# Ten modulation units of a two-layer diffusion block: column layout and VectorE sums in place of float32 products

## The chip, the cores and the metric

One Trainium2 chip, one core of it. The metric is the device time of one execution in microseconds; the kernel before takes 1705.74 us, the median of 3 runs (1704.96 to 1706.06). Five engines work side by side, each through its own queue in order: TensorE (matrix products; PE in the profile, its weight loads PEld), VectorE (DVE), ScalarE (ACT), GpSimd (POOL) and SyncE (SP), which here issues every load from HBM.

## What is computed

Two layers of a hybrid diffusion block on 256 latent tokens and 256 context tokens of width 1024. In each layer a vector c (and another one, c_ctx, for the context) gives six shift, scale and gate vectors of width 1024:

```python
c_act = jax.nn.silu(c)
cc_act = jax.nn.silu(c_ctx)
sh1, sc1, g1, sh2, sc2, g2 = jnp.split((c_act @ ada_w[i] + ada_b[i])[:, None, :], N_ADA, axis=-1)
csh1, csc1, cg1, csh2, csc2, cg2 = jnp.split(cc_act @ ada_w[i] + ada_b[i], N_ADA, axis=-1)
...
x_new = x + g1 * merge_groups(p, attn, *group_w)
x_new = x_new + g2 * ffn(modulate(x_new, norm2_g[i], sh2, sc2))
```

Normalized and modulated tokens pass one input projection, whose columns go to four mixers (a chunked spatial gate, pooling, attention with low-rank queries and keys, a Fourier mixer); their outputs are projected back and added with the gate g1. A second normalization, modulated with sh2 and sc2, feeds a dense SwiGLU in layer 0 and a SwiGLU with the best 2 of 8 experts in layer 1, added with g2. Context is carried through layer 0 only. `ada_w` is 1024x6144 float32 per layer, multiplied by two vectors.

## The kernel before, in words

Everything is float32. Large products are made as three products of float32r halves (`mm3`, lines 245 to 248): a weight tile is split into a high part, copied by ScalarE (line 236), and a low part, subtracted by VectorE (line 238). There are three pairs of split tiles in layer 0, and three raw tiles of 1 MB (`raw_unit`, line 229) into which SyncE loads weights in turn.

**The modulation.** `ada_w` of a layer is cut into 24 units of 256 columns, 1 MB each. Units 0 to 7 are sh1 and sc1, 8 to 11 g1, 12 to 15 sh2, 16 to 19 sc2, 20 to 23 g2. In layer 0 a unit is `ada0_unit` (lines 348 to 360): eight float32 products of 32x256, whose weights are 32 columns with c and c_ctx in the first two (`c32`), in four groups of rows of one PSUM bank (line 353); a copy to SBUF on ScalarE (356); two products with a selecting matrix that add the groups and turn the result to columns (358); a small bias add on VectorE (359). Each float32 product shows as two records in the trace. The tile comes from `ada0_load` (332 to 346): among units 8 to 19 the odd ones take a raw tile, the even ones a tile of their own, `aw` (line 815), loaded at line 345; units 20 to 23 take the one buffer `rx` (`ada_raw`, line 838).

In layer 1 a unit is `ada1_unit` (856 to 866). Its weights are laid out with output columns on partitions. `cast_c` (847 to 854) writes c and c_ctx, repeated on all partitions, into `cb` by 16 transposes of broadcast columns (852) and four copies. One VectorE instruction then multiplies a 128x1024 half of a unit by one of the two vectors and sums along the row into one column of `ada` (863): four for units 0 to 7, two for the others, which need no context. Their products go to a throw-away tile `junk`. A small add of the bias follows (866).

**Order of the work.** The program text gives a list; a planner simulates the engines and sets the order on each of them, by priority, which is by default the place in the text, raised where `high_priority` or `pri` stands. In layer 0 units 0 to 7 belong to the first normalization. Then come key and query preparation, `aw`, and a `merge` (line 818) of the latent attention's steps, at raised priority, with a list of other work: units 8 and 9, the input projections `w0_v` and `w0_u`, units 10 and 11, the gate, `w0_z`, `w0_d`, the Fourier mixer, units 12 and 13, 16 to 19, the context's queries, 14 and 15, pooling. The output projections `wout` follow, for the latents and then for the context beside its attention. The dense feed-forward (`ffn`, 868) runs over 14 chunks of 256 hidden columns, for the latents and then for the context; a chunk has 96 products for gate and up and 48 for the chunk before going down. In the first run `cast_c` is hung on chunk 0, units 20 to 23 on chunks 3 to 6, and layer 1's units 0 to 7 on chunks 3 to 10; layer 1's other units are hung on the second run. Small tiles come from pools with a set number of buffers (`temps`; `sm`), among them `t1` (normalized values, squares, the units' copies), `rs`, `gs` and `mx`.

Layer 1's mixers and its experts follow; the experts' weights, 336 units of 1 MB, make up the last half of the time. Their first loads go to tiles that layer 1 sets free.

Of the kernel before, what the change touches and what calls it, by code (L numbers as in the profile page):

```python
# [10 lines left out]
F32 = mybir.dt.float32  # L11
# [87 lines left out]
def _layout(i):  # L99
# [5 lines left out]
    for l in range(2):  # L105
# [54 lines left out]
        else:  # L160
            w = w.reshape(4, 2, 128, 1024)[[3, 0, 1, 2]].transpose(0, 2, 1, 3)
        a[f"wout{l}"] = w.reshape(4, 128, 2048)
    a["ada0"] = i["ada_w"][0].reshape(8, 128, 24, 256).transpose(2, 1, 0, 3).reshape(24, 128, 2048)
    a["ada1"] = i["ada_w"][1].T.reshape(24, 2, 128, 1024).transpose(0, 2, 1, 3).reshape(24, 128, 2048)

    def units(g, u, d, fm):
# [18 lines left out]
def build(tc, I, out):  # L185
# [125 lines left out]
    def t4(name, shape=(128, 4, 256)):  # L311
        return tt("t4", name, shape)
# [14 lines left out]
        return TB(name, shape)  # L327

    adaw = {}
    aw = None  # L330

    def ada0_load(u, tiles=None):

        if tiles is None:
            if u < 20:
                tiles = [raw_unit(I["ada0"][u])] if u < 8 or u % 2 else [aw]
            else:
                tiles = [ada_raw(I["ada0"][u])]
            load = u > 7 and u < 20 and u % 2 == 0
        else:  # L340
            load = True
        n = 2048 // len(tiles)
        if load:
            for i, t in enumerate(tiles):
                nc.sync.dma_start(t, I["ada0"][u][:, i * n:i * n + n])
        return [t[:, a:a + 256] for t in tiles for a in range(0, n, 256)]

    def ada0_unit(u):
# [8 lines left out]
        for m in range(2):  # L357
            PE.matmul(ps[:, 256 + 2 * m:258 + 2 * m], sb[:, m * 128:m * 128 + 128], C("sel", 0, 2), start=True, stop=True)
        V.tensor_tensor(out=ada[0][:, 2 * u:2 * u + 2, :], in0=ps[:, 256:260].rearrange("p (m i) -> p m i", m=2),
                        in1=ps_(0, "adab", 2 * u, 2)[:, :, None].to_broadcast([128, 2, 2]), op=ALU.add)  # L360

    def rstd(ss, n, dim):
        ms = sm.tile([128, 8], F32, tag="ms", name="ms")
        V.tensor_scalar(ms[:, :n], ss, 1.0 / dim, EPS, op0=ALU.mult, op1=ALU.add)
        r = sm.tile([128, 8], F32, tag="rs", bufs=12, name="rs")
        G.tensor_tensor(out=r[:, :n], in0=ms[:, :n], in1=C("neghalf", 0, n), op=ALU.pow)
        return r

# [26 lines left out]

    def modulate(l, n, jsh, jsc, s, R, kts, hi, lo=None):
        a, w = kts[0], len(kts)
        g = sm.tile([128, 8], F32, tag="gs", bufs=6, name="gs")
        V.scalar_tensor_tensor(g[:, :w], ada[l][:, jsc * 8 + a:jsc * 8 + a + w, s], 1.0, ps_(l, n, a, w), op0=ALU.add,
                               op1=ALU.mult)  # L400
        for i, kt in enumerate(kts):
            t_ = t1("nm")
            V.scalar_tensor_tensor(t_, xs[s][:, kt], g[:, i:i + 1], R, op0=ALU.mult, op1=ALU.mult)
            sh = adav(l, jsh, kt, s)
            S.activation(hi[:, kt], t_, AF.Identity, bias=sh)
            if lo is not None:
                V.scalar_tensor_tensor(lo[:, kt], t_, sh, hi[:, kt].bitcast(F32), op0=ALU.add, op1=ALU.subtract)
# [127 lines left out]
    def attend(st, keys):  # L535

        nk = 2 * len(keys)
        pts = {}

        def soft(h, t):  # L540
            sc = PSC()
            for i, ks in enumerate(keys):
                PE.matmul(sc[:, i * 256:i * 256 + 256], st.qT[:, h, t * 128:t * 128 + 128], ks.kT[:, h, :],
                          start=True, stop=True)
            m = sm.tile([128, 6], F32, tag="mx", bufs=6, name="mx")
            V.tensor_reduce(out=m[:, 0:1], in_=sc[:, :nk * 128], axis=AX.X, op=ALU.max, negate=True)
            p = tb("p")
            S.activation(p[:, :nk * 128], sc[:, :nk * 128], AF.Exp, bias=m[:, 0:1], accum_out=m[:, 1:2])
            V.reciprocal(m[:, 2:3], m[:, 1:2])
            V.tensor_scalar(p[:, :nk * 128], p[:, :nk * 128], m[:, 2:3], None, op0=ALU.mult)  # L550
            tr = PTR()
            for k in range(nk):
                PE.transpose(tr[:, k * 128:k * 128 + 128], p[:, k * 128:k * 128 + 128], ident)
            pts[h] = tb("pt", (128, 4, 128))
            S.activation(pts[h][:, :nk], tr.rearrange("p (k q) -> p k q", k=4)[:, :nk], AF.Copy)

        def soft2(pr, t):

            sc = PSC()
            for j in range(2):  # L560
                PE.matmul(sc[:, j * 256:j * 256 + 256], st.qT[:, 2 * pr + j, t * 128:t * 128 + 128],
                          keys[0].kT[:, 2 * pr + j, :], start=True, stop=True)
            m = sm.tile([128, 6], F32, tag="mx", bufs=6, name="mx")
            V.tensor_reduce(out=m[:, 0:2], in_=sc.rearrange("p (j k) -> p j k", j=2), axis=AX.X, op=ALU.max,
                            negate=True)
            p = tb("p")
            for j in range(2):
                a = slice(j * 256, j * 256 + 256)
                S.activation(p[:, a], sc[:, a], AF.Exp, bias=m[:, j:j + 1], accum_out=m[:, 2 + j:3 + j])
            V.reciprocal(m[:, 4:6], m[:, 2:4])  # L570
            p2 = p.rearrange("p (j k) -> p j k", j=2)
            V.tensor_tensor(out=p2, in0=p2, in1=m[:, 4:6, None].to_broadcast([128, 2, 256]), op=ALU.mult)
            tr = PTR()
            for k in range(4):
                PE.transpose(tr[:, k * 128:k * 128 + 128], p[:, k * 128:k * 128 + 128], ident)
            pt = tb("pt", (128, 4, 128))
            S.activation(pt.rearrange("p k q -> p (k q)"), tr, AF.Copy)
            for j in range(2):
                pts[2 * pr + j] = pt[:, 2 * j:2 * j + 2]

        def mix(pr, t):
            o = PTR()
            for k in range(nk):
                v = keys[k // 2].v
                for j in range(2):
                    h = 2 * pr + j
                    PE.matmul(o[64 * j:64 * j + 64, :128], v[:, k % 2, h * 64:h * 64 + 64], pts[h][:, k, :],
                              start=k == 0, stop=k == nk - 1, tile_position=(0, 64 * j))
# [145 lines left out]
    NPRE = 3  # L734


    temps("tp0", t4=3, t3=3, t2=8, t1=4, ta=6, tb=3, v=2, R=2)
    TB = lambda name, shape: tt("tb", name, shape)
    weights("w0", 3, 3)
    pb, pb_close = pool("pb", bufs=2, space=PSUM)  # L740
# [71 lines left out]
    q_in0(0, x_, pcq, 0)  # L812
    q_in0(0, c_, pcq, 256)
    q_up(0, x_, True)
    aw = t8("aw", F32, (128, 2048))
    new_mix(x_)
    ada0s = lambda *us: lambda: [ada0_unit(u) for u in us]
    merge(pri(1000, attend(x_, [x_, c_])),
          [ada0s(8, 9), w0_v, w0_u, ada0s(10, 11), lambda: gate_mix(0, x_), w0_z, w0_d, lambda: fourier_mix(0, x_),
           ada0s(12, 13), ada0s(16, 17, 18, 19), lambda: q_up(0, c_, False), ada0s(14, 15), lambda: pool_mix(0, x_)])  # L820
# [9 lines left out]
    pq_close()  # L830


    temps("tp1", t4=3, t3=2, t2=6, t1=3, ta=5, v=2, R=1)
    rx, rx_close = pool("rx", bufs=1, side="left")

    def ada_raw(src):
        r = rx.tile([128, 2048], F32, tag="rx", bufs=1, name="rx")
        nc.sync.dma_start(r, src)
        return r
# [2 lines left out]
    pq, pq_close = pool("pq1", bufs=1, space=PSUM)  # L842
    PW = lambda: pq.tile([128, 512], F32, tag="gu", bufs=2, name="gu")
    fp, fp_close = pool("fp", bufs=2, side="right")
    cb = t8("cb", F32, (128, 2, 1024))

    def cast_c():
        for i in range(2):
            for k4 in range(2):
                ps = PS()  # L850
                for k in range(4):
                    PE.transpose(ps[:, k * 128:k * 128 + 128],
                                 c32[:, k4 * 4 + k, i:i + 1].to_broadcast([128, 128]), ident)
                S.activation(cb[:, i, k4 * 512:k4 * 512 + 512], ps, AF.Copy)

    def ada1_unit(u):

        r = (raw_unit if u > 14 else ada_raw)(I["ada1"][u]).rearrange("p (m k) -> p m k", m=2)
        n = 2 if u < 8 else 1
        for m in range(2):  # L860
            for i in range(n):
                j = r[:, m] if n == 1 else t4("junk", (128, 1024))
                V.scalar_tensor_tensor(j, r[:, m], 1.0, cb[:, i], op0=ALU.mult, op1=ALU.mult,
                                       accum_out=ada[1][:, 2 * u + m, i:i + 1])
        a = ada[1][:, 2 * u:2 * u + 2, :n]
        V.tensor_tensor(out=a, in0=a, in1=ps_(1, "adab", 2 * u, 2)[:, :, None].to_broadcast([128, 2, n]), op=ALU.add)

    def ffn(s, fhl, extra):
        fh, fl = fhl
# [48 lines left out]
    ex0[1] += pri(100, [norm2_c])  # L918
    ex0[0].append(cast_c)
    for u in range(4):  # L920
        ex0[3 + u].append(lambda u=u: ada0_unit(20 + u))
    for u in range(8):
        ex0[3 + u].append(lambda u=u: ada1_unit(u))
    ffn(0, fhl, ex0)
# [573 lines left out]
```

## Time and profile before

| | |
|---|---|
| median of 3 runs | 1705.74 us (1704.96 to 1706.06) |
| the profiled execution | 1704.32 us |
| its span in the trace | 1702.5 us |
| mean granted clock of TensorE | 0.991 of full speed |
| busy: TensorE, its weight loads | 1637.2 us (96%), 1248.4 us (73%) |
| busy: VectorE, ScalarE, GpSimd | 854.0 us (50%), 645.2 us (38%), 32.2 us (2%) |
| chain that ended last | TensorE 76%, transfers 19%, VectorE 3%, ScalarE 1% |

The span is what the trace covers; the execution's own time lies 1.8 us above it. Busy shares are of the whole span and mix stages. Matmuls overlap in the engine's pipeline: a product of 256 columns has a duration of 0.28 us and more, but the next one begins 0.12 us after it, so that costs are read from one start to the next, from the chain, or from counts in a stretch. The same holds in a small measure for VectorE.

### The profile page before, as it was taken

Reading aid. Unit: us, or ns where it says so; the run is one execution under the profiler, and the core shown is the slowest. Engines: PE = TensorE matmul, PEld = TensorE weight load, DVE = VectorE, ACT = ScalarE, POOL = GpSimd, SP = SyncE. Lnnn points to the kernel's source line nnn. Section 1 sums busy time; section 2 is a strip of 40 time slices with the busy share of each in tenths; the row PEclk is TensorE's granted clock in tenths of the full one; section 3 lists DMA queues with packets and bytes.
Section 4 is the critical chain, followed back from the end, with each engine's and each line's share of the span. In section 5 each row is a group of like instructions: output and inputs, shape, how many; then the busy total and the mean of one; then the engine's idle time right before and its main releaser. Section 6 shows DMA issues by size and latency. Waiting matters only on the chain.

```text
span 1702.5 us, 28623 instructions
## 1 busy us (share of the span) xinstructions
PE 1637.2 (96%) x11648; PEld 1248.4 (73%) x11648; DVE 854.0 (50%) x1446; ACT 645.2 (38%) x1026; POOL 32.2 (2%) x31
## 2 busy tenths in 40 slices
PE   7999999999999999999899999999999999989996
PEld 4887889999999999999776555555565655545543
DVE  3545666688766666657673334334343424233411
ACT  4434464444454444455472223223232323222200
POOL 0100000000000000000100000000000000000000
PEclk9999999999999999999999999999999999999999
DMA  9425346778744566654479999999999999999996
GB/s 374 171 100 199 136 174 219 276 278 300 268 170 161 198 248 242 246 186 168 173 298 380 420 418 419 419 418 419 416 418 420 418 417 419 419 419 418 419 418 259
DMA packets 77901, 525.26 MB, mean 309 GB/s; under 512 B 9024, under 2 KB 9152, under 8 KB 18240
## 3 DMA queue, kind: packets, MB, share of 16 engines
q1 hardware_dynamic: 77760, 523.33, 77.5%
q8 instruction: 94, 1.54, 0.4%
q14 instruction: 47, 0.39, 0.1%
HBM read 522.25 MB, written 1.05 MB: 307 GB/s over the span
## 4 chain that ended last, share of the span: by engine, by line
PE 76%; DMA 19%; DVE 3%; ACT 1%; issue 1%; SPq 0%; POOL 0%; DVEq 0%; ACTq 0%; POOLq 0%
PE gu L1395 11%; DMA raw<-in_moe 9%; PE gu L247 9%; PE gu L246 9%; PE gu L248 9%; PE ys L1381 5%; DMA prb<-in_moe 5%; PE acc L247 4%; PE acc L246 4%; PE acc L248 4%; DMA x<-in_moe 2%; PE w L246 2%; PE w L248 2%; PE w L247 2%; PE yd L247 1%; DMA spare<-in_moe 1%
## 5 line engine op out<-in xcount | busy, mean ns | idle before, releaser
L238 DVE TENSOR_TENSOR wl<-raw,wh 128x1024 fp32r<-128x1024 f32 x368 | 446.3, 1223 | 221.8 <-ACT wh L236 215.3
L236 ACT ACTIVATE wh<-raw 128x1024 fp32r<-128x1024 f32 x368 | 384.8, 1057 | 330.5 <-PE gu L247 149.8
L246 PE MATMUL gu<-fh,wh 128*128 128x256 f32 x896 | 254.1, 284 | 0.0
L248 PE MATMUL gu<-fh,wl 128*128 128x256 f32 x896 | 251.3, 281 | 0.0
L247 PE MATMUL gu<-fl,wh 128*128 128x256 f32 x896 | 250.9, 280 | 0.0
L1395 PE MATMUL gu<-raw,es 128*64 128x256 f32 x1488 | 181.3, 383 | 5.0 <-DMA raw<-in_moe 4.8
L1398 ACT ACTIVATE sg<-gu 64x256 f32<-64x256 f32 x84 | 31.6, 376 | 394.8 <-PE gu L1395 388.7
L246 PEld LDWEIGHTS gu<-fh,wh 128*128 128x128 f32 x896 | 168.1, 188 | 4.7 <-issue 4.7
L247 PEld LDWEIGHTS gu<-fl,wh 128*128 128x128 f32 x896 | 168.6, 188 | 2.7 <-issue 2.7
L248 PEld LDWEIGHTS gu<-fh,wl 128*128 128x128 f32 x896 | 168.8, 189 | 1.8 <-issue 1.6
L1399 DVE TENSOR_TENSOR sg<-sg,gu 64x256 f32<-64x256 f32 x84 | 35.7, 424 | 254.1 <-ACT sg L1398 253.7
L1395 PEld LDWEIGHTS gu<-raw,es 128*64 128x64 f32 x1488 | 105.5, 137 | 64.5 <-issue 11.2
L247 PE MATMUL acc<-hl,wh 128*128 128x256 f32 x448 | 124.5, 283 | 0.0
L246 PE MATMUL acc<-hh,wh 128*128 128x256 f32 x448 | 123.8, 283 | 0.0
L248 PE MATMUL acc<-hh,wl 128*128 128x256 f32 x448 | 120.3, 283 | 0.0
L1381 PE MATMUL ys<-raw,hs 128*64 128x512 f32 x424 | 103.6, 603 | 7.3 <-DMA raw<-in_moe 6.1
L247 PE MATMUL gu<-wl,ef 128*128 128x512 f32 x224 | 94.9, 424 | 8.2 <-DVE wl L238 8.1
L246 PE MATMUL gu<-wh,ef 128*128 128x512 f32 x224 | 93.4, 418 | 8.2 <-ACT wh L236 8.2
L248 PE MATMUL gu<-wh,ef 128*128 128x512 f32 x224 | 90.3, 403 | 0.0
L247 PEld LDWEIGHTS acc<-hl,wh 128*128 128x128 f32 x448 | 85.7, 191 | 0.0
L246 PEld LDWEIGHTS acc<-hh,wh 128*128 128x128 f32 x448 | 85.6, 191 | 0.0
L248 PEld LDWEIGHTS acc<-hh,wl 128*128 128x128 f32 x448 | 83.3, 191 | 0.0
(448 smaller groups left out, 2521.9 us busy)
## 6 DMA issues: line engine op xcount, KB each, us to landing
raw<-in_moe SPq DMA_DIRECT2D x223, 1024.0 KB, 17.4
raw<-in_ffn SPq DMA_DIRECT2D x84, 1024.0 KB, 4.9
spare<-in_moe SPq DMA_DIRECT2D x31, 1024.0 KB, 18.2
x<-in_moe SPq DMA_DIRECT2D x28, 1024.0 KB, 19.8
prb<-in_moe SPq DMA_DIRECT2D x27, 1024.0 KB, 18.0
rx<-in_ada SPq DMA_DIRECT2D x19, 1024.0 KB, 4.9
raw<-in_ada SPq DMA_DIRECT2D x18, 1024.0 KB, 4.8
cst<-in_moe SPq DMA_DIRECT2D x27, 512.0 KB, 18.0
```

The source lines that it names most:

```text
L236: S.activation(hi, r, AF.Copy)
L238: V.tensor_tensor(out=lo, in0=r, in1=hi.bitcast(F32), op=ALU.subtract)
L246: PE.matmul(o, wh, rh, start=start, stop=False, **kw)
L247: PE.matmul(o, wh, rl, start=False, stop=False, **kw)
L248: PE.matmul(o, wl, rh, start=False, stop=stop, **kw)
L1381: PE.matmul(yd[0][64 * q:64 * q + 64, :], h[:, m * 64:m * 64 + 64], rs[m][:, q * 512:q * 512 + 512], start=c == 0 and m == 0, stop=c == NC ...
L1395: PE.matmul(ps[64 * q:64 * q + 64, :256], st.e[:, kt], rs[k // 2][:, a:a + 256], start=kt == 0, stop=kt == 7, tile_position=(0, 64 * q))
L1398: S.activation(g[64:], ps[:64, :256], AF.Silu)
L1399: V.tensor_tensor(out=g[64:], in0=g[64:], in1=ps[64:, :256], op=ALU.mult)
```

## The change

Units 8 to 13 and 20 to 23 of layer 0 are laid out by column, as layer 1's are, and computed as those are. The function of layer 1 becomes `ada_cols`, for both layers. Units 14 to 19 stay as they were, and so do 0 to 7. `cast_c` moves up to the place where `aw` was taken, and writes a `cb` tile there; it is still hung on chunk 0 of the feed-forward too, where it takes a new `cb` tile and writes it again. `aw` is gone: units 8 to 19 all take raw tiles. In the mixing stage `junk` has one buffer of its own (`jk`), and there are fewer buffers of `t1`, `rs`, `gs` and `mx`.

```diff
-    a["ada0"] = i["ada_w"][0].reshape(8, 128, 24, 256).transpose(2, 1, 0, 3).reshape(24, 128, 2048)
+    a["ada0"] = np.concatenate(
+        [i["ada_w"][0][:, :2048].reshape(8, 128, 8, 256).transpose(2, 1, 0, 3).reshape(8, 128, 2048),
+         i["ada_w"][0][:, 2048:].T.reshape(16, 2, 128, 1024).transpose(0, 2, 1, 3).reshape(16, 128, 2048)])
+    for u in range(14, 20):
+        a["ada0"][u] = i["ada_w"][0][:, 256 * u:256 * u + 256].reshape(8, 128, 256).transpose(1, 0, 2).reshape(128, 2048)
...
         if tiles is None:
-            if u < 20:
-                tiles = [raw_unit(I["ada0"][u])] if u < 8 or u % 2 else [aw]
-            else:
-                tiles = [ada_raw(I["ada0"][u])]
-            load = u > 7 and u < 20 and u % 2 == 0
+            tiles = [raw_unit(I["ada0"][u])]
...
+    def ada_cols(l, u, src, n):
+        r = src.rearrange("p (m k) -> p m k", m=2)
+        e = V if l == 0 else V
+        for m in range(2):
+            for i in range(n):
+                j = r[:, m] if i == n - 1 else tt(JUNK[0], "junk", (128, 1024))
+                e.scalar_tensor_tensor(j, r[:, m], 1.0, cb[0][:, i], op0=ALU.mult, op1=ALU.mult,
+                                       accum_out=ada[l][:, 2 * u + m, i:i + 1])
+        a = ada[l][:, 2 * u:2 * u + 2, :n]
+        e.tensor_tensor(out=a, in0=a, in1=ps_(l, "adab", 2 * u, 2)[:, :, None].to_broadcast([128, 2, n]), op=ALU.add)
...
-        r = sm.tile([128, 8], F32, tag="rs", bufs=12, name="rs")
+        r = sm.tile([128, 8], F32, tag="rs", bufs=8, name="rs")
...
-        g = sm.tile([128, 8], F32, tag="gs", bufs=6, name="gs")
+        g = sm.tile([128, 8], F32, tag="gs", bufs=4, name="gs")
...
-            m = sm.tile([128, 6], F32, tag="mx", bufs=6, name="mx")
+            m = sm.tile([128, 6], F32, tag="mx", bufs=4, name="mx")
...
-    temps("tp0", t4=3, t3=3, t2=8, t1=4, ta=6, tb=3, v=2, R=2)
+    temps("tp0", jk=1, t4=3, t3=3, t2=8, t1=3, ta=6, tb=3, v=2, R=2)
...
-    aw = t8("aw", F32, (128, 2048))
+    cb = []
+    def cast_c():
+        cb[:] = [t8("cb", F32, (128, 2, 1024))]
...
+    cast_c()
     new_mix(x_)
-    ada0s = lambda *us: lambda: [ada0_unit(u) for u in us]
+    ada0s = lambda *us: lambda: [ada_cols(0, u, raw_unit(I["ada0"][u]), 2) if u < 14 else ada0_unit(u) for u in us]
...
+    JUNK[0] = "t4"
...
     for u in range(4):
-        ex0[3 + u].append(lambda u=u: ada0_unit(20 + u))
+        ex0[3 + u].append(lambda u=u: ada_cols(0, 20 + u, ada_raw(I["ada0"][20 + u]), 2))
```

## Rows read from the trace of the kernel before

**Rows 1.** Table by stretches of the span; the first line names the columns.

```profile
core 0: us, PE busy (x) PEld busy (x) DVE busy (x) ACT busy (x) POOL busy (x), PEclk, DMA share, GB/s
0.00:30.00 30.00, 18.07 (x146) 10.02 (x147) 8.83 (x25) 14.40 (x35) 2.21 (x5) 0.96 0.91 359
...
80.00:130.00 50.00, 50.00 (x404) 44.67 (x403) 20.35 (x53) 18.11 (x38) 3.73 (x4) 1.00 0.23 85
130.00:160.00 30.00, 29.71 (x258) 19.75 (x257) 15.78 (x40) 15.10 (x32) 0.59 (x1) 1.00 0.66 244
...
283.00:358.00 75.00, 75.00 (x658) 72.13 (x658) 52.95 (x80) 31.58 (x44) 0.00 (x0) 1.00 0.75 281
358.00:400.00 42.00, 42.00 (x355) 41.85 (x354) 38.54 (x61) 18.61 (x24) 0.00 (x0) 1.00 0.67 248
...
850.00:1702.50 852.50, 806.58 (x4884) 482.64 (x4882) 314.55 (x496) 242.32 (x356) 0.00 (x0) 0.99 0.98 402
```

**Rows 2.** Chain of waits, first 300 us: start, us, engine, tile, line, count.

```profile
44.77 1.64 DVE nm L403 x4
...
95.59 1.86 PE w L353 x32
99.54 0.34 PE w L358 x4
...
146.77 0.42 DVE df L656
...
150.01 0.61 DVE mx L546
...
229.28 0.87 PE b L852 x8
```

**Rows 3.** Waits of TensorE, 50 to 215 us: us in total, times, longest.

```profile
PE w L358 <- ACT adasb L356: 0.8, 2, 0.5
```

**Rows 4.** Instructions in order of time, VectorE, feed-forward of layer 0: start, duration.

```profile
289.60 1.22 DVE L863 SCALAR_TENSOR_TENSOR junk<-rx,cb 128x1024 f32<-128x1024 f32 x1
...
290.74 1.22 DVE L863 SCALAR_TENSOR_TENSOR junk<-rx,cb 128x1024 f32<-128x1024 f32 x1
...
294.18 1.22 DVE L238 TENSOR_TENSOR wl<-raw,wh 128x1024 fp32r<-128x1024 f32 x1
295.32 0.41 DVE L898 TENSOR_TENSOR sg<-sg,gu 128x256 f32<-128x256 f32 x1
295.65 1.22 DVE L238 TENSOR_TENSOR wl<-raw,wh 128x1024 fp32r<-128x1024 f32 x1
...
306.46 0.16 DVE L359 TENSOR_TENSOR ada<-gu,prs 128x4 f32<-128x4 f32 x1 [2.09 <-PE gu L358]
...
325.21 0.16 DVE L359 TENSOR_TENSOR ada<-gu,prs 128x4 f32<-128x4 f32 x1 [2.09 <-PE gu L358]
...
356.85 1.22 DVE L863 SCALAR_TENSOR_TENSOR junk<-rx,cb 128x1024 f32<-128x1024 f32 x1 [1.38 <-DMA rx<-in_ada]
```

**Rows 5.** Instructions in order of time, SyncE's queue of loads.

```profile
34.24 18.68 SPq L229 DMA_DIRECT2D raw<-in_win  x2
...
62.38 13.36 SPq L229 DMA_DIRECT2D raw<-in_win  x2
...
373.97 0.33 SPq L838 DMA_DIRECT2D rx<-in_ada  x1
...
385.29 0.33 SPq L838 DMA_DIRECT2D rx<-in_ada  x1
```

**Rows 6.** Instructions in order of time, VectorE, mixing stage of layer 0.

```profile
69.94 0.48 DVE L520 TENSOR_SCALAR v<-b,rs 128x256 f32<-128x256 f32 x1 [5.23 <-ACT k L518]
...
74.16 1.23 DVE L238 TENSOR_TENSOR wl<-raw,wh 128x1024 fp32r<-128x1024 f32 x1 [1.38 <-ACT wh L236]
...
96.60 1.23 DVE L238 TENSOR_TENSOR wl<-raw,wh 128x1024 fp32r<-128x1024 f32 x1
```

**Rows 7.** Loads by line, first 300 us: count, KB, median us to landing.

```profile
raw<-in_win SPq DMA_DIRECT2D x4, 1024.0 KB, 5.9
```

More of the change, by code (lines that the diff above doesn't have):

```diff
@@ L329, in build @@
     adaw = {}
-    aw = None
     def ada0_load(u, tiles=None):
         if tiles is None:
-            if u < 20:
-                tiles = [raw_unit(I["ada0"][u])] if u < 8 or u % 2 else [aw]
-            else:
-                tiles = [ada_raw(I["ada0"][u])]
-            load = u > 7 and u < 20 and u % 2 == 0
-        else:
-            load = True
-        n = 2048 // len(tiles)
-        if load:
+            tiles = [raw_unit(I["ada0"][u])]
+        else:
+            n = 2048 // len(tiles)
             for i, t in enumerate(tiles):
                 nc.sync.dma_start(t, I["ada0"][u][:, i * n:i * n + n])
+        n = 2048 // len(tiles)
         return [t[:, a:a + 256] for t in tiles for a in range(0, n, 256)]
@@ L360, in ada0_unit @@
                         in1=ps_(0, "adab", 2 * u, 2)[:, :, None].to_broadcast([128, 2, 2]), op=ALU.add)
+    JUNK = ["jk"]
+    def ada_cols(l, u, src, n):
[8 more added lines that the diff above has]
+        e.tensor_tensor(out=a, in0=a, in1=ps_(l, "adab", 2 * u, 2)[:, :, None].to_broadcast([128, 2, n]), op=ALU.add)
     def rstd(ss, n, dim):
@@ L562, in soft2 @@
                           keys[0].kT[:, 2 * pr + j, :], start=True, stop=True)
-            m = sm.tile([128, 6], F32, tag="mx", bufs=6, name="mx")
+            m = sm.tile([128, 6], F32, tag="mx", bufs=4, name="mx")
             V.tensor_reduce(out=m[:, 0:2], in_=sc.rearrange("p (j k) -> p j k", j=2), axis=AX.X, op=ALU.max,
@@ L814, in build @@
     q_up(0, x_, True)
-    aw = t8("aw", F32, (128, 2048))
+    cb = []
+    def cast_c():
+        cb[:] = [t8("cb", F32, (128, 2, 1024))]
+        for i in range(2):
+            for k4 in range(2):
+                ps = PS()
+                for k in range(4):
+                    PE.transpose(ps[:, k * 128:k * 128 + 128],
+                                 c32[:, k4 * 4 + k, i:i + 1].to_broadcast([128, 128]), ident)
+                S.activation(cb[0][:, i, k4 * 512:k4 * 512 + 512], ps, AF.Copy)
+    cast_c()
     new_mix(x_)
-    ada0s = lambda *us: lambda: [ada0_unit(u) for u in us]
+    ada0s = lambda *us: lambda: [ada_cols(0, u, raw_unit(I["ada0"][u]), 2) if u < 14 else ada0_unit(u) for u in us]
     merge(pri(1000, attend(x_, [x_, c_])),
@@ L844, in build @@
     fp, fp_close = pool("fp", bufs=2, side="right")
[L845 to L854, printed above, removed]
-    def ada1_unit(u):
[L858 to L866, printed above, removed]
+    def ada1_unit(u):
+        ada_cols(1, u, (raw_unit if u > 14 else ada_raw)(I["ada1"][u]), 2 if u < 8 else 1)
     def ffn(s, fhl, extra):
```

## The prediction

> **What bounds the kernel now.** I read the page first: TensorE is busy for 96% of the span, and the work that ended last runs through it. Then the table by stretches, because one average hides several stages. In it the reader is to see that from 80 to 130 us TensorE is busy 50.00 of 50 us and from 283 to 400 us all the time, at a granted clock of 1.00 (the 2.4 GHz level), while VectorE has 20.35 of 50 us in the first of these and 38.54 of 42 us in the last [rows 1]. From 850 us on it is the other way round: transfers run at 402 GB/s with a share of 0.98 [rows 1]. That last stage reads a fixed amount of expert weights, and its buffers come free when layer 1 ends; so what the earlier stages save moves its start, and with it its end. TensorE's time before 850 us therefore counts one for one, unless what replaces it makes TensorE wait.
>
> Next the chain of waits: in layer 0 it is a string of TensorE pieces in which the modulation units stand with their own time, broken by VectorE pieces between 146.77 and 150.6 us [rows 2]. TensorE's only recorded wait between 50 and 215 us is 0.8 us, for the copy inside a modulation unit [rows 3].
>
> **What goes from TensorE, feed-forward of layer 0.** Four units (20 to 23), one per chunk. VectorE's small bias add of such a unit starts at 306.46 and at 325.21 us, so a chunk with a unit takes 18.75 us [rows 4]. A chunk has 144 other products (96 for gate and up, 48 for down); from 358 to 400 us 355 products took 42.00 us, 0.1183 us each [rows 1], so a chunk without a unit takes 17.04. The unit costs 1.71 us, four cost **6.8 us**. This includes the change between kinds of product.
>
> **What goes from TensorE, mixing stage of layer 0.** Six units (8 to 13). The chain has 1.86 us for the first part of two units and 0.34 for the second part of one [rows 2], 1.27 us a unit; with up to 0.44 for changing kinds of product it would be the 1.71 of the feed-forward. These units partly stand between other float32 work, so I take 1.4: **8.4 us**, with 7.6 and 10.3 as ends.
>
> **What is added on TensorE.** The broadcast of c is now written twice: once more in layer 0, 16 transposes. The existing one has 0.87 us for 8 [rows 2], so **1.75 us** more, all of it counted, although some may fall into the first 30 us, where TensorE is busy only 18.07 [rows 1]. Its copies on ScalarE lie beside TensorE, and the six units' copies that go away there are more in number than the four added.
>
> **What is added on VectorE.** Four multiply-and-sum passes of 128x1024 per unit: one starts at 289.60, the next at 290.74 us [rows 4], 1.14 us apart, and the small add is there before as after; about 4.7 us a unit, 28 us for the six and 19 for the four. Nothing of it is on the path as long as VectorE has room. In layer 0 it has: idle 29.65 us from 80 to 130 and 14.2 from 130 to 160 [rows 1]. In the feed-forward it is close. A chunk's own VectorE work is six splits at 1.14 us [rows 4] and four passes over 256 columns at 0.33 [rows 4], 8.2 us; two units beside it make 17.6 against 17.04. But both units go through one buffer, rx, and its loads follow each other at 373.97 and 385.29 us, 11.3 apart [rows 5]: 4.7 in 11.3 plus 8.2 in 17.04 is 0.90 of VectorE. From 358 to 400 us the trace shows just this density, 38.54 of 42 us, with TensorE at 42.00 of 42 [rows 1]. And since TensorE's turn no longer paces the buffer, the four units can start before chunk 3. So I cost this at **0**; the cover is the set of three split tiles ahead of TensorE, 2.8 us of products each. If it is gone, every us by which a split is late is a us of TensorE.
>
> **The loads.** Units 8, 10, 12, 14, 16 and 18 had a tile of their own (aw); now all of 8 to 19 and the input weights share three raw tiles. The load that waits is SyncE's, and all loads queue behind it. Before, the second of the two win0 loads that begin at 34.24 us came only 18.68 us later, the second of those at 62.38 us 13.36 later [rows 5]; tiles loaded early lay there long, as the splits at 74.16 and 96.60 us show [rows 6]. A unit's tile is free once VectorE has read it, and VectorE sat idle for 5.23 us before 69.94 us [rows 6]. I cost the ring at 0, with the upper end under the rivals.
>
> **The smaller pools.** t1 has three buffers instead of four in layer 0. At 44.77 us four nm passes follow each other in 1.64 us [rows 2]; with three buffers the fourth goes behind the first xl pass, on the same engine. Between 0 and 0.41 us for each of three such groups, 1.2 us; I take 0, since VectorE merely changes the order. rs, gs and mx hold values that are used up by the time of their reuse: 0 to 0.41 us, taken as 0.
>
> **An allowance.** From 130 to 160 us, where units 12 and 13 run, VectorE pieces stand in the chain [rows 2], and attention goes step by step through VectorE. TensorE is busy 29.71 of 30 us there, but its weight loads only 19.75, against 44.67 of 50 in the stretch before [rows 1]. Some of that is shorter loads for narrow tiles; some may be filler that hides a chain. I let half of these two units' 2.8 us go: **1.4 us**. The Trainium skill, page "Perfetto Trace Analysis", section "Identifying the Most-Contended Engine", says that matmul busy time is no good measure of how near TensorE is to its limit and that the busy share of the weight loads is one; by that rule this stretch has slack, all 2.8 us would be lost, and the sum would be 1.4 us smaller; where it is full, in the feed-forward, the rule agrees with the trace (41.85 of 42 us).
>
> **The sum.** -6.8 - 8.4 + 1.75 + 1.4 = -12.05 us. The profiled execution took 1704.32 us (a span of 1702.5 and 1.8 around it), 1.4 below the median of the runs shown. So 1692.3 for that execution, 1693.7 against the median. A measurement of this kernel can tell about 0.2%, 3.4 us, from no change.
>
> **Rivals.** (B) *The mixing stage gives nothing.* If attention's steps and the transfers set its pace, TensorE's 7 us there become waiting, and the broadcast shows. For it: VectorE's pieces in the chain [rows 2]. Against it: one wait of TensorE, 0.8 us in all [rows 3]. Time: 1705.7 - 6.8 + 1.75 = 1700.7.
>
> (C) *VectorE becomes the bound in the feed-forward.* If the planner keeps two units in each of chunks 3 to 6, a chunk needs 17.6 us of VectorE; and a unit whose load has not landed holds up the splits behind it, as at 356.85 us for 1.38 us [rows 4]. With two such waits a chunk takes 20.4 us against 18.75 before: 6.6 us lost for 6.8 hoped for, and 1705.7 - 8.4 + 1.4 + 1.75 + 6.6 = 1707. With fewer waits it goes over into the forecast; about half of the case lies below 1704. Against it: 0.92 of VectorE with TensorE full from 358 to 400 us [rows 1].
>
> (D) *The three raw tiles starve the mixing stage,* and it ends slower. The loads of win0 units u, z and d wait for a tile that VectorE must first read for a modulation unit, which needs the broadcast first, and SyncE's queue stands meanwhile. A late unit costs its landing, 5.9 us [rows 7], and the first split, 1.14: 7.0 us if TensorE has nothing else. Three of them: 1693.7 + 21 = 1714.7. It decides the sign from 4 us a unit. For it: SyncE's loads already wait long for tiles [rows 5], and modulation is late in VectorE's priorities. Against it: before, the weights lay ready long before their splits [rows 6], and VectorE has gaps.
>
> That the change does nothing on TensorE can be left out: ten units are gone from it by the code; 14 to 19 stay.
>
> **How the numbers follow.** Forecast 0.67, with a range of its own from 1690 (six units at 1.71, no allowance, the broadcast partly hidden) to 1697; B 0.11; C 0.09; D 0.13. The predicted time is the forecast's, 1693.7. From 1690 to 1704 the range takes in B and the better half of C, and leaves out D and the rest of C, 0.17 in all. Faster: forecast and B, 0.78; same: C, 0.09; slower: D, 0.13.
>
> **What would show it.** Chunks of the feed-forward at 17.0 us with the products of the units gone; column passes starting before 283 us, some 11 us apart through rx; TensorE still full from 80 to 130 us and from 283 to 400; the last stage starting 12 us earlier and unchanged in length. Wrong would be: waits of TensorE on the split tiles near 283 to 400 us (C), on raw tiles between 60 and 110 us (D), or gaps of 5 us or more between 130 and 160 us (B).

## The result, and the profile after

The changed kernel takes 1725.24 us (median of 4 runs, 1722.51 to 1726.55) where the kernel before takes 1705.72 beside it: a ratio of 1.0116 with an interval of 1.0104 to 1.0128, slower by 1.2%. The forecast was 1693.7 with a range from 1690 to 1704: the time lies outside it and on the other side. The profiled execution is the one of 1722.51 us (span 1720.7, mean granted clock 0.984).

First the table by stretches of the changed kernel, columns as in [rows 1].

```profile
0.00:30.00 30.00, 19.06 (x163) 10.18 (x163) 8.24 (x24) 14.11 (x32) 2.12 (x5) 1.00 0.92 359
80.00:130.00 50.00, 32.03 (x182) 27.30 (x182) 32.75 (x68) 15.55 (x26) 3.69 (x4) 0.76 0.26 93
130.00:160.00 30.00, 30.00 (x262) 25.15 (x260) 17.22 (x41) 8.50 (x20) 0.00 (x0) 1.00 0.53 193
283.00:358.00 75.00, 74.66 (x629) 74.46 (x629) 69.53 (x113) 36.54 (x52) 0.00 (x0) 1.00 0.69 259
358.00:400.00 42.00, 42.00 (x357) 42.00 (x356) 39.11 (x62) 18.42 (x25) 0.00 (x0) 1.00 0.74 280
850.00:1702.50 852.50, 812.29 (x4933) 489.32 (x4931) 321.29 (x530) 248.82 (x370) 4.93 (x5) 0.99 0.98 402
```

One stretch has broken: from 80 to 130 us TensorE ran 404 products before [rows 1] and runs 182 now, and the granted clock is 0.76 where it was 1.00. In the feed-forward TensorE is as full as before (74.66 of 75 us) with VectorE at 69.53, as forecast. The last stage has its old share and rate (0.98, 402 GB/s): it starts later and is not longer.

The broken stretch in finer steps:

```profile
90.00:100.00 10.00, 1.87 (x9) 1.14 (x9) 4.99 (x15) 1.97 (x4) 2.29 (x2) 0.64 0.00 0
100.00:110.00 10.00, 5.09 (x27) 4.43 (x25) 7.47 (x12) 5.42 (x9) 0.00 (x0) 0.84 0.08 13
110.00:115.00 5.00, 0.71 (x4) 0.72 (x5) 5.00 (x13) 0.00 (x0) 0.00 (x0) 0.50 0.65 239
115.00:120.00 5.00, 4.85 (x14) 3.55 (x13) 4.96 (x10) 2.96 (x4) 0.00 (x0) 0.50 0.57 203
120.00:125.00 5.00, 4.52 (x27) 4.22 (x27) 5.00 (x10) 1.48 (x3) 0.00 (x0) 0.64 0.64 236
125.00:130.00 5.00, 5.00 (x45) 5.00 (x44) 5.00 (x10) 1.06 (x1) 0.00 (x0) 1.00 0.62 229
```

From 90 to 115 us TensorE is busy for 7.67 of 25 us. From 110 to 120 us the granted clock is 0.50, the 1.2 GHz level; the 14 products from 115 us on take 4.85 us, and only from 125 us on is the clock back at 1.00. What TensorE waits for from 50 to 215 us, to be held against the single 0.8 us of [rows 3]:

```profile
PE b L566 <- DVE p L563: 9.2, 1, 9.2
PE b L521 <- DVE q L511: 8.1, 1, 8.1
PE b L521 <- DVE q L497: 1.9, 1, 1.9
```

There are two holes. In the first, up to 99.45 us, TensorE stands before the queries' transposes (L521); in the second, up to 114.29 us, before a transpose in the latent attention (L566). Why TensorE had no other work meanwhile stands in SyncE's queue, to be read beside [rows 5]:

```profile
32.20 1.00 SPq L234 DMA_DIRECT2D raw<-in_ada  x2
49.85 10.12 SPq L234 DMA_DIRECT2D raw<-in_win  x2
67.99 40.88 SPq L234 DMA_DIRECT2D raw<-in_ada  x2
112.71 5.50 SPq L234 DMA_DIRECT2D raw<-in_win  x2
122.57 17.96 SPq L234 DMA_DIRECT2D raw<-in_ada  x5
```

Units 8 and 9 are loaded from 32.20 us, unit 10 at 67.99: these are three raw tiles, all there are, and none is read yet. The load of unit 11 then waits until 108.9 us, 40.88 us after the pair began, and the input projections `w0_z` and `w0_d`, queued behind it, start at 112.71. The chain of waits (start, us, engine, tile, line) says what they wait for:

```profile
99.45 0.64 PE b L521 x2
100.08 1.72 PE b L836 x8
101.83 0.61 ACT cb L838
102.46 1.25 DVE junk L370 x2
...
113.83 0.40 DVE p L563
...
117.86 1.15 DVE junk L370 x2
...
119.61 1.14 DVE wl L243
```

L836 is the broadcast of c. It stands on TensorE behind the queries' transposes, these wait for the queries' normalization on VectorE, and so the first pass of a unit (L370) begins at 102.46 us. The tiles come free in the passes that follow. From there to 119.6 us the chain runs through these passes: the second hole ends with attention's step `p` (L563), which VectorE does at 113.83 us between passes, and VectorE is busy without a break from 105 to 115 us.

Where stages are compared below, **mixing end** is the start of the last addition of `wout`'s result to x, and **feed-forward end** the start of the first addition after the latents' feed-forward. The kernel before has them at 232.8 and 481.7 us, the changed kernel at 251.1 and 496.9: +18.3 and +15.2, and the span ends +18.2. Each comes from one profiled execution; the kernels before and of e2_ffn_only, whose mixing stages differ in nothing of the program, have the mixing end 1.0 us apart, and a control below moves it by 2.4 us without a reason, so that differences of one or two microseconds tell nothing.

### The profile page after: what moved, and what is told of

It is laid out like the page before. It is cut to its first block, busy times and chain, and to the rows that moved or that the text cites. A ratio compares the mean times of both kernels' runs of the same rounds, so it can differ in the third digit from the quotient of the medians.

```text
span 1720.7 us, 28330 instructions
## 1 busy us (share of the span) xinstructions
PE 1632.6 (95%) x11464; PEld 1246.0 (72%) x11464; DVE 897.5 (52%) x1526; ACT 646.4 (38%) x1020; POOL 31.9 (2%) x31
## 4 chain that ended last, share of the span: by engine, by line
PE 70%; DMA 22%; DVE 5%; ACT 1%; issue 1%; POOL 0%; SPq 0%; DVEq 0%; ACTq 0%; POOLq 0%
DMA raw<-in_moe 11%; PE gu L1401 9%; PE gu L252 8%; PE gu L251 8%; PE gu L253 8%; DMA prb<-in_moe 7%; PE acc L252 4%; PE acc L251 4%; PE acc L253 4%; PE ys L1387 4%; DMA x<-in_moe 2%; PE w L252 2%; PE w L253 2%; PE w L251 2%; DVE wl L243 1%; DMA spare<-in_moe 1%
```

## The experiments

The expectations use these letters. **T**: the broadcast stands too late on TensorE, the units hold the raw tiles until it is there, and the loads behind them starve TensorE. **V**: VectorE's passes crowd the short steps of keys, queries and attention, wherever they stand. **F**: the freed products were filler that covered such steps, so that freeing them gains little. Later **P**, the smaller pools, and **Q**, a better place for the context's queries, were added.

Rows in this table: time (median, us), ratio to the kernel before with its 95% interval, and both points against 232.8 and 481.7 us.

| run | time | ratio | mixing end | feed-forward end |
|---|---|---|---|---|
| changed kernel | 1725.24 | 1.0116 [1.0104, 1.0128] | +18.3 | +15.2 |
| e2_ffn_only | 1700.85 | 0.9972 [0.9962, 0.9982] | +1.0 | -6.3 |
| e3_mix_only | 1731.28 | 1.0156 [1.0139, 1.0173] | +18.1 | +21.8 |
| e1_cb_early | 1714.82 | 1.0062 [1.0043, 1.0080] | +9.8 | +7.0 |
| e4_order | 1724.38 | 1.0114 [1.0096, 1.0132] | +20.6 | +18.0 |
| e11_q_up_first | 1721.79 | 1.0104 [1.0085, 1.0123] | +14.0 | +11.3 |
| e7_no_aw | 1710.31 | 1.0025 [1.0016, 1.0035] | +0.5 | +1.4 |
| e8_small_pools | 1711.56 | 1.0036 [1.0023, 1.0048] | +4.4 | +6.5 |
| e9_t1_only | 1712.65 | 1.0040 [1.0029, 1.0051] | +5.3 | +7.9 |
| e10_sm_only | 1704.86 | 0.9997 [0.9988, 1.0007] | -0.7 | -0.4 |
| e12_psum_turn | 1709.30 | 1.0025 [1.0015, 1.0036] | -2.4 | -2.5 |
| e13_pools_back | 1716.38 | 1.0063 [1.0044, 1.0083] | +16.2 | +7.7 |
| e14_early_pools | 1708.66 | 1.0018 [1.0008, 1.0028] | +6.3 | -1.4 |

Four more runs (e5, e6, e15, e16) leave out sums of the modulation. Their experts are then chosen otherwise and the last stage takes another way (3883 to 3908 us), so they are read at the mixing end alone.

**Which half of the change.** e2_ffn_only is the kernel before with units 20 to 23 alone by column; e3_mix_only is the changed kernel with those four back on TensorE.

```diff
-    for u in range(14, 20):
+    for u in (*range(14, 20), *range(20, 24)):
...
-        ex0[3 + u].append(lambda u=u: ada_cols(0, 20 + u, ada_raw(I["ada0"][20 + u]), 2))
+        ex0[3 + u].append(lambda u=u: ada0_unit(20 + u))
```

(This is e3; e2 is the same idea from the other kernel, with `aw`, the pools and the one broadcast left as they were before.)

> The kernel before with units 20 to 23 alone by column on VectorE; the mixing stage is that of before, and c is broadcast once. Theory T: the feed-forward part of the change is a gain of its own, of 4.9 us (what the changed kernel regains between the first chunk's gate and the feed-forward's end) to 6.8 us (the prediction's term): 1699 to 1701 us. Rival F (VectorE bounds the feed-forward): 1707 us or more. Rival V says nothing on it.

> The changed kernel with units 20 to 23 back on TensorE as float32 products; units 8 to 13 stay on VectorE with the late broadcast. Theory T and rival V: the whole loss is in the mixing stage, so that this one is slower than the changed kernel by the feed-forward's 5 to 7 us: 1729 to 1733 us. Rival F: 1700 us or less.

Measured: e2 1700.85 us, 4.9 below the kernel before and the fastest of the study; e3 1731.28. At the feed-forward end e2 stands 6.3 us early, and e3 6.6 us behind the changed kernel. So the four units are worth what was forecast for them (6.8), and the loss lies in the mixing stage. The table by stretches of e2:

```profile
283.00:358.00 75.00, 75.00 (x631) 74.85 (x630) 68.03 (x106) 32.82 (x43) 0.00 (x0) 1.00 0.73 274
358.00:400.00 42.00, 42.00 (x356) 42.00 (x355) 34.24 (x53) 18.94 (x26) 0.00 (x0) 1.00 0.82 324
```

TensorE is full at the full clock, as in [rows 1], with VectorE at 0.91.

**The late broadcast.** e1_cb_early moves the broadcast up in the text, behind the first normalization. e4_order leaves it and puts the units that need it behind the Fourier mixer, so that `w0_z` and `w0_d` are queued ahead of them.

```diff
+    cb = []
+
+    def cast_c():
+        cb[:] = [t8("cb", F32, (128, 2, 1024))]
...
+    cast_c()
...
-    cast_c()
```

```diff
-          [ada0s(8, 9), w0_v, w0_u, ada0s(10, 11), lambda: gate_mix(0, x_), w0_z, w0_d, lambda: fourier_mix(0, x_),
-           ada0s(12, 13), ada0s(16, 17, 18, 19), lambda: q_up(0, c_, False), ada0s(14, 15), lambda: pool_mix(0, x_)])
+          [w0_v, w0_u, lambda: gate_mix(0, x_), w0_z, w0_d, lambda: fourier_mix(0, x_),
+           ada0s(8, 9), ada0s(10, 11), ada0s(12, 13), ada0s(16, 17, 18, 19), lambda: q_up(0, c_, False), ada0s(14, 15), lambda: pool_mix(0, x_)])
```

> The changed kernel with the first broadcast of c moved up in the text, behind the loop of the first normalization; nothing else differs. Theory T (the broadcast comes late: its transposes stand on TensorE behind the queries' transposes and end at about 102 us, until then units 8 to 10 hold all three raw tiles and the loads of w0_z and w0_d queue behind them): the mixing stage is full again and the time is 1693 to 1701 us, with column passes on VectorE from about 55 us and the load of w0_z before 85 us. Rival V (the six units' passes on VectorE crowd attention's steps, wherever the broadcast stands): 1715 us or more. Rival F (the feed-forward lost the time): 1720 us or more, as the changed kernel.

> The changed kernel with units 8 to 11 moved in the list of the mixing stage from between the input projections to behind the Fourier mixer, ahead of 12 and 13; the broadcast keeps its place in the text. Theory T: the input weights take the raw tiles first, nothing waits for the broadcast, and the time is 1693 to 1703 us although the passes come late. Rival V: the same passes lie even closer to attention's steps, 1715 us or more.

e1 took 1714.82 us, between what the theories give: it takes back 10.4 us of the loss of 19.5, and 8.5 of 18.3 at the mixing end. The hole from 90 to 120 us is gone, but VectorE is now full while keys and queries are prepared (stretches of e1):

```profile
60.00:70.00 10.00, 10.00 (x63) 7.86 (x64) 9.97 (x21) 5.83 (x10) 1.40 (x2) 1.00 0.60 208
70.00:80.00 10.00, 10.00 (x87) 10.00 (x86) 10.00 (x19) 3.42 (x8) 3.91 (x2) 1.00 0.50 189
80.00:90.00 10.00, 10.00 (x87) 10.00 (x87) 9.59 (x22) 5.24 (x9) 0.00 (x0) 1.00 0.50 180
...
120.00:130.00 10.00, 6.31 (x19) 4.29 (x18) 3.28 (x7) 2.69 (x8) 0.00 (x0) 0.61 0.28 107
```

The first maximum of the latent attention starts at 120.1 us where it started at 107.3 in the kernel before. TensorE has done the projections meanwhile, is busy for 6.31 of the 10 us that follow, and the clock falls there.

e4 took 1724.38 us against the 1693 to 1703 expected by the theory that the ring alone was at fault: that theory fell as the whole account. It holds for the first hole: with `w0_z` and `w0_d` loaded in time, TensorE is full where it was busy for 1.87 of 10 us, although the passes begin at 106 us, no earlier than before. e4's stretch from 90 to 100 us, and its waits of TensorE from 50 to 215 us:

```profile
90.00:100.00 10.00, 10.00 (x85) 10.00 (x86) 7.41 (x17) 2.92 (x5) 2.30 (x2) 1.00 0.00 0
```

```profile
PE b L566 <- DVE p L563: 10.6, 3, 6.2
PE b L521 <- DVE q L497: 6.0, 1, 6.0
```

The ring is clear, yet the passes, now between 106 and 140 us, stand on VectorE in front of the attention's steps. In every place that was tried for the six units' passes in this stage, a chain of short steps waits.

e11_q_up_first, on top of e1, brings the context's queries forward, to give TensorE work in e1's later holes.

```diff
-           ada0s(12, 13), ada0s(16, 17, 18, 19), lambda: q_up(0, c_, False), ada0s(14, 15), lambda: pool_mix(0, x_)])
+           lambda: q_up(0, c_, False), ada0s(12, 13), ada0s(16, 17, 18, 19), ada0s(14, 15), lambda: pool_mix(0, x_)])
```

> The kernel of the early broadcast with the context's queries moved ahead of units 12 and 13 and 16 to 19 in the list of the mixing stage. Theory Q (with ten units gone, TensorE has too little other work in its queue between the queries' products and their transposes, and the next entry waits for VectorE; now 33 entries of the plan stand between them where 25 did): 1705 to 1711 us, TensorE's wait for q below 2 us. Rival V (the passes on VectorE are all that is left): 1713 to 1717 us, no change.

It took 1721.79 us, 7.0 more than e1. TensorE's wait for `q` is 2.1 us where it was 3.5 in e1, but its waits for attention's `p` are 7.5 in all where they were 3.7. The theory behind it fell, and no better order was found.

**The pools and the prefetch tile, in the kernel before.** e7_no_aw takes `aw` away, e8_small_pools makes all four pools smaller, e9_t1_only `t1` alone, e10_sm_only the other three.

```diff
-    temps("tp0", t4=3, t3=3, t2=8, t1=4, ta=6, tb=3, v=2, R=2)
+    temps("tp0", t4=3, t3=3, t2=8, t1=3, ta=6, tb=3, v=2, R=2)
```

> The kernel before, all units on TensorE, with aw taken away: units 8 to 19 all go through the three raw tiles. Theory T2: a unit that TensorE reads is done with its tile in about 1 us, so 1704 to 1708 us, no change. Rival R: 1712 us or more.

> The kernel before with the smaller pools of the change alone (t1 of the mixing stage 3 for 4, rs 8 for 12, gs 4 for 6, mx 4 for 6). Theory T2 and the prediction: 0 to 2 us, 1704 to 1708 us. Rival R: 1710 us or more.

> The kernel before with t1 of the mixing stage at 3 buffers for 4, and nothing else. Together with the run of the small counters alone it tells which pool made the smaller pools cost 6 us. Theory P (a copy of a modulation unit, a square or a normalized value waits for one of three buffers): 1709 to 1713 us. Rival N (any change of the plan moves the time by some us, whichever pool it is): anywhere from 1703 to 1713 us, and the other run like it.

> The kernel before with rs 8 for 12, gs 4 for 6 and mx 4 for 6, and t1 left at 4. Theory P: these values are used up by the time their buffers are reused, 1704 to 1707 us. Rival N: anywhere from 1703 to 1713 us.

The three small pools cost nothing (1704.86 us). One buffer less of `t1` costs 0.40% (0.29 to 0.51), about 6.9 us, and accounts for all of e8. In the first normalization the trace shows how. The kernel before, then e9:

```profile
27.39 1.67 DVE L403 SCALAR_TENSOR_TENSOR nm<-x,gs,R 128x256 f32<-128x256 f32 x4
29.69 1.68 DVE L407 SCALAR_TENSOR_TENSOR xl<-nm,ada,xh 128x256 fp32r<-128x256 f32 x4 [0.62 <-ACT xh L405]
```

```profile
28.44 1.27 DVE L403 SCALAR_TENSOR_TENSOR nm<-x,gs,R 128x256 f32<-128x256 f32 x3
31.25 0.88 DVE L407 SCALAR_TENSOR_TENSOR xl<-nm,ada,xh 128x256 fp32r<-128x256 f32 x2 [1.55 <-ACT xh L405]
32.05 0.48 DVE L403 SCALAR_TENSOR_TENSOR nm<-x,gs,R 128x256 f32<-128x256 f32 x1
32.45 0.48 DVE L407 SCALAR_TENSOR_TENSOR xl<-nm,ada,xh 128x256 fp32r<-128x256 f32 x1
33.10 0.48 DVE L407 SCALAR_TENSOR_TENSOR xl<-nm,ada,xh 128x256 fp32r<-128x256 f32 x1 [0.18 <-ACT xh L405]
```

With three buffers the fourth normalized value (`nm`) has to wait until ScalarE has made `xh` and VectorE `xl` from the first, and VectorE idles for ScalarE meanwhile: the four take 5.1 us where they took 4.0. The first normalization ends 2.0 us later, and the first maximum of the latent attention starts 2.5 us later (109.8 against 107.3 us). By the code the copies of modulation units have no part in this stretch: those of units 0 to 7 lie in `ta`, and only the later units' in `t1`. The rest of the 5.3 us at the mixing end is in the main one wait of TensorE, at 153 us, that the kernel before does not have:

```profile
PE w L353 <- DMA aw<-in_ada: 3.2, 1, 3.2
```

It is a wait for a unit's load; whether it comes from the pool or from another order of the plan was not tried. The loss of `aw` (e7) costs 0.25% in time, between what its two theories gave, though only 0.5 us at the mixing end. Of its 4.9 us at the end of the span, 3.5 arise behind the feed-forward's end. There the kernel before takes 1220.8 us to the end of the span, and every other kernel of the table between 1222.1 and 1225.3.

e13_pools_back and e14_early_pools test the same in the changed kernel and in e1: all four pools as before, with a 2-byte throw-away tile to make room.

```diff
-                j = r[:, m] if i == n - 1 else tt(JUNK[0], "junk", (128, 1024))
+                j = r[:, m] if i == n - 1 else tt(JUNK[0], "junk", (128, 1024), F32 if JUNK[0] == "t4" else mybir.dt.bfloat16)
...
-    temps("tp0", jk=1, t4=3, t3=3, t2=8, t1=3, ta=6, tb=3, v=2, R=2)
+    temps("tp0", jk=1, t4=3, t3=3, t2=8, t1=4, ta=6, tb=3, v=2, R=2)
```

> The changed kernel with t1, rs, gs and mx at the sizes of before; the room comes from the throw-away tile, which is now bfloat16. Theory P (three buffers of t1 cost 5 to 8 us as in the kernel before, beside the late broadcast): 1716 to 1720 us. Rival N (the 5 to 8 us belong to the plan of the kernel before alone and do not add): 1722 to 1727 us.

> The kernel of the early broadcast with t1, rs, gs and mx at the sizes of before and the throw-away tile in bfloat16. Theory P: 1706 to 1710 us. Rival N: 1712 to 1718 us.

P's ranges held: they come out 8.9 us below the changed kernel and 6.2 below e1. Broadcast and pools together bring it to 1708.66 us, 1.0018 of the kernel before: 16.6 of the 19.5 us lost. That is still 7.8 us above e2, which leaves the six units on TensorE. Between the mixing end and the feed-forward end, e14 needs 241.2 us against 246.1 in e1, e13 240.4 against 245.8 in the changed kernel, and e9 251.5 against 248.9 in the kernel before; so a third to over two thirds of what the pools cost up to the feed-forward end arises behind the mixing end. Why is open: `t1` has three buffers in the feed-forward of every kernel here.

**A control.** e12_psum_turn is the kernel before with the turn of its PSUM banks begun at 4, a change without a reason of its own, made because every edit also gives the planner another order.

```diff
+    turn[0] = 4
```

> The kernel before with the turn among PSUM buffers begun 4 later, as the four copies of the broadcast leave it; work, tiles and pools are the same. It measures what a plan that differs without a reason is worth. Theory T2: 1703 to 1708 us. Rival N: 1709 us or more, or 1701 us or less.

It took 1709.30 us, 0.25% more (0.15 to 0.36), although it was 2.5 us early at both points. (Its profiled execution was its shortest, 1706.27 us.) So a difference of some 4 us may be the plan's alone, and e7's 0.25% can't be told from that. The cost of `t1` (6.9 us) lies above it, and giving the pools back gained 8.9 and 6.2 us in two other kernels.

**Freed products against VectorE's passes.** e15_units_gone is the kernel before without the products and copies of units 8 to 13: what is freed, with nothing in its place. e5_short_late, e6_short_early and e16_short_back are the changed kernel, e1 and e14 with each pass of units 8 to 13 over 8 of 1024 columns: number and waits as before, the time nearly gone (0.16 us for 1.22). Units 20 to 23 keep whole passes, so the expectation of e16 is wrong where it speaks of ten units.

```diff
+        if 8 <= u < 14:
+            V.tensor_tensor(out=ada[0][:, 2 * u:2 * u + 2, :], in0=r[0][:, 0:4].rearrange("p (m i) -> p m i", m=2),
+                            in1=ps_(0, "adab", 2 * u, 2)[:, :, None].to_broadcast([128, 2, 2]), op=ALU.add)
+            return
```

```diff
-                e.scalar_tensor_tensor(j, r[:, m], 1.0, cb[0][:, i], op0=ALU.mult, op1=ALU.mult,
+                w = 8 if l == 0 and u < 14 else 1024
+                e.scalar_tensor_tensor(j[:, :w], r[:, m, :w], 1.0, cb[0][:, i, :w], op0=ALU.mult, op1=ALU.mult,
```

> The changed kernel with the passes of units 8 to 13 cut from 1024 to 8 columns each (it leaves out all but 8 terms of these units' sums), the broadcast as late as in the changed kernel; loads, tiles and waits stay. Theory T2 (two causes: the raw tiles are held until the late broadcast, and the 24 passes of 1.15 us crowd the chain of keys, queries and attention on VectorE, early or late): only the first is left, the gap of TensorE between about 91 and 105 us stays and the time is 1704 to 1716 us. Rival H (the held tiles are all of it): as the changed kernel, 1720 us or more. Rival C (VectorE's passes are all of it): 1692 to 1699 us.

> The kernel of the early broadcast with the passes of units 8 to 13 cut to 8 columns each (it leaves out all but 8 terms of these units' sums). Theory T2: neither cause is left and the time is the prediction's, 1691 to 1697 us; the 1715 us of the early broadcast with whole passes is then VectorE's. Rival R (the lost aw tile, the changed order of loads or the smaller pools cost what remains): 1705 us or more.

> The kernel before with units 8 to 13 left out of the sums (their loads stay, VectorE reads four columns of each and adds the bias; their products with c are left out on every engine). The time at the end then depends on other routing, so the reading is the end of the mixing stage, the last addition of wout, at 232.8 us in the kernel before. The prediction's term (TensorE is full, so 8.4 us less of products is 8.4 us of time): 223.5 to 225.5 us. Rival B and theory F (these products were filler that covered waits of the attention steps and of the context's queries): 229 to 234 us.

> The kernel of e14 (broadcast early, pools of before) with each VectorE pass over 8 columns of the 1024 instead of all: the passes keep their number and their waits but lose nearly all of their time. Most of the ten units' sums are left out, the bias alone remains nearly whole, so the routing changes and the end of the run is not compared; read is the end of the mixing stage (the last addition of the output projection to x), 239.1 us in e14 and 227.3 us in the kernel of before with the units' products gone. If the time of the passes on VectorE is what lies between the two (11.8 us): 228 to 232 us. If it is the eight transposes, the lost prefetch tile and another order of the planned steps: 236 to 240 us.

| run | mixing end, us | against before |
|---|---|---|
| e5_short_late | 242.6 | +9.8 |
| e6_short_early | 239.1 | +6.3 |
| e15_units_gone | 227.3 | -5.5 |
| e16_short_back | 236.0 | +3.2 |

e15: freeing the six units' products is worth 5.5 us and not 8.4, although nothing takes their place; that is between what the prediction's term and F expected. In its stretch from 130 to 160 us,

```profile
130.00:160.00 30.00, 26.67 (x176) 19.11 (x176) 16.35 (x40) 12.98 (x28) 2.53 (x2) 0.96 0.37 139
```

TensorE is idle for 3.3 us where it was idle for 0.29 [rows 1].

e5 keeps the late broadcast. Of TensorE's two long waits in the changed kernel the first stays as it was, and the second, for attention's `p`, shrinks from 9.2 us:

```profile
PE b L522 <- DVE q L512: 8.1, 1, 8.1
PE b L567 <- DVE p L564: 2.6, 1, 2.6
```

So the first hole belongs to the broadcast and the loads, the second in the main to the passes. In e6 both causes are gone, and the stage, with the small pools, is still 6.3 us late. The passes' time is worth 8.5 us in the changed kernel (251.1 to 242.6), where they stand in front of the raw tiles, and 3.1 us in e14 (239.1 to 236.0, just inside what was expected if the passes are not the cause, and little more than the control's 2.4). The rest, 236.0 against 227.3, is 8.7 us that neither passes nor pools explain. e16's one long wait of TensorE and the stretch in which it lies:

```profile
PE b L522 <- DVE q L498: 5.8, 1, 5.8
```

```profile
150.00:160.00 10.00, 6.89 (x48) 4.79 (x46) 2.00 (x6) 2.88 (x5) 1.49 (x1) 0.93 0.01 2
160.00:170.00 10.00, 6.64 (x20) 4.97 (x21) 4.18 (x8) 2.38 (x6) 0.81 (x2) 0.50 0.00 0
```

Here TensorE waits for the context's queries, no transfer runs, and the clock is down. TensorE is full from 100 to 130 us; a reading is that the planner has spent its other work there, and that the products that could cover this wait are gone. The wait and the clock are seen; that another order would mend it was not shown, since the other orders tried (e4, e11) gave no gain or were slower.

## Why the prediction was wrong, point by point

- **Feed-forward, -6.8: right.** 6.3 (e2) and 6.6 (e3 against the changed kernel) at the feed-forward end; 4.9 us of it reach the end of e2. Passes that meet an unlanded `rx` (on VectorE, below) wait 0.3 to 1.1 us without harm to TensorE, so the cover of three split tiles held: from 245 to 500 us TensorE waits for a split once, for 0.3 us.

```profile
312.33 1.23 DVE L370 SCALAR_TENSOR_TENSOR junk<-rx,cb 128x1024 f32<-128x1024 f32 x1 [1.12 <-DMA rx<-in_ada]
...
323.27 1.23 DVE L370 SCALAR_TENSOR_TENSOR junk<-rx,cb 128x1024 f32<-128x1024 f32 x1 [0.31 <-DMA rx<-in_ada]
...
334.19 1.23 DVE L370 SCALAR_TENSOR_TENSOR junk<-rx,cb 128x1024 f32<-128x1024 f32 x1 [0.45 <-DMA rx<-in_ada]
```

  There the units follow each other 10.9 us apart (323.27 less 312.33), where 11.3 was read from [rows 5]; the four before them, from 253.44 us on, came 14 to 19 us apart.
- **The loads, "I cost the ring at 0": wrong, the step that failed first.** The prediction knew that a tile is free once VectorE has read it, and took VectorE's idle time [rows 6] as proof that it would read soon. But the reading needed the broadcast, the broadcast needed TensorE's queue, and there it stood behind the queries. The idle 5.23 us of VectorE was no cover for work that had no operand. Instead of 0, TensorE stood for 8.1 us in the first hole, which is gone in e1 and e4 and stays in e5. Moving the broadcast (e1) takes 8.5 us of the 18.3 away at the mixing end; with the passes short already it takes 3.5 (e5 against e6), so the two causes can't be added up.
- **Rival D named this mechanism** ("needs the broadcast first, and SyncE's queue stands meanwhile") and its sign, with 1714.7 us. Its place was right. Its price, 21 us for three late units, is not what the runs give for this cause alone (8.5 us); the measured time lies above D's since other terms failed beside it. TensorE was idle for 18 of the 50 us, at a granted clock of 0.76 in the stretch, which D did not count.
- **The smaller pools, "I take 0": wrong for `t1`.** It took it that VectorE merely changes the order of its passes. But a buffer is free only when ScalarE, too, has read it, and VectorE stood for that. Bounds 0 to 1.2 us; the first normalization alone ended 2.0 us later, and the whole cost was 6.9 in the kernel before, 8.9 and 6.2 in the two later ones. For `rs`, `gs` and `mx` the 0 was right (0.9997).
- **VectorE's passes, 0 in the mixing stage: wrong.** Idle time of 29.65 of 50 us [rows 1] did not hide them: 8.5 us in the changed kernel (e5), where they stand in front of tiles and make most of the second hole of 9.2 us. In e14 it is 3.1, hardly clear of the control. They are 1.14 us each, in front of steps of 0.16 to 0.7 us on which TensorE waits.
- **Six units, -8.4 with an allowance of 1.4: perhaps too much by 1.5 us.** e15 gives -5.5 against -7.0. The allowance was half of units 12 and 13's 2.8 us; all of it would have given -5.6. That is what followed from the Trainium skill, page "Perfetto Trace Analysis", section "Identifying the Most-Contended Engine" (the weight loads' busy share, not the matmuls', tells how near TensorE is to its limit). e15 lies nearer to it, but the 1.5 us are less than the control's 2.4, so no run here decides it.
- **The second broadcast, +1.75: too little where it stood.** The 1.72 us in the chain above are 8 of its 16 transposes, for which the prediction had 0.87; the granted clock there was 0.50 from 95 to 100 us and 0.69 from 100 to 105. In e1, away from the hole, 14 of the 16 took 1.5 us (from 47.17 us to the next product at 48.66), as counted. Its place mattered more than its length.
- **"What the earlier stages save moves the last stage": right**, with the sign turned: +15.2 us at the feed-forward end, +18.2 at the end of the span, and the last stage at its old rate. Of the 3.0 us between, 1.8 arise ahead of the last stage's first gate. They belong to no part of this change alone: the control, too, takes 4.5 us longer than the kernel before from the feed-forward's end on.

The parts, from e15 at -5.5 us: 8.7 for the rest of the mixing stage (order, transposes, `aw`), 3.1 for the passes, 3.5 for the pools up to there (e14 to e1), 8.5 for the late broadcast, in all +18.3 at the mixing end. These sizes hold for this order of taking things away: in the changed kernel the pools are worth 2.1 us there (e13) and the passes 8.5 (e5). Of the 8.7 only the wait in e16 is seen; its cause is open.

## What to carry to other kernels

Before work is moved to an engine with idle time, follow its operands back through every queue that makes them: here an idle VectorE could not start since eight transposes stood late on TensorE, and three load buffers were held the while. For a pool, ask which engines must have read a buffer before it is free, and which engine stands meanwhile. And products that look like pure cost may be the cover of a chain of short steps: in this kernel the conversion paid where TensorE was full on its own (the feed-forward, 4.9 us gained), and not beside attention.

## What the runs showed of the hardware beyond expectation

In this stage the holes on TensorE cost more than their length. With TensorE busy for 1.87 of 10 us the granted clock was 0.64, and 0.50 from 110 to 120 us; products behind the second hole then ran at the 1.2 GHz level, 0.21 us from one start to the next where it is 0.12 at 124.75 us:

```profile
121.39 0.41 PE L252 MATMUL w<-xl,wh 128*128 128x256 f32 x1
121.60 0.41 PE L253 MATMUL w<-xh,wl 128*128 128x256 f32 x1
...
124.75 0.28 PE L251 MATMUL w<-xh,wh 128*128 128x256 f32 x1
124.87 0.28 PE L252 MATMUL w<-xl,wh 128*128 128x256 f32 x1
```

The clock was low again in e1 (0.61 from 120 to 130 us) and e16 (0.50 from 160 to 170). Not every hole did it: from 180 to 190 us the changed kernel's TensorE is busy for 7.47 of 10 us at 1.00. In the kernel before, the clock was 1.00 from 80 to 160 us [rows 1].
